# A fixed opening order in which every read of one PSUM bank comes ahead of the tile that takes the bank over

## The chip, the cores and the metric

The kernel runs on one core of one Trainium2 chip. The metric is device time in microseconds (us) of one execution, by the median of several runs. The core has a matmul engine (PE, with PEld for its weight loads), a vector engine (DVE), an activation engine (ACT), GpSimd (POOL) and SyncE (SP), which here only issues DMAs. Each engine works its own instructions off in the order of the program and stops at an instruction whose inputs are not there yet.

## The reference

Two decoder layers over 512 tokens of width 1024. Each layer is a SwiGLU feed-forward half step, a token mixer (windowed attention, RWKV-7 and a short convolution side by side) and a second feed-forward half step. Each of the six sub-layers starts from a normalised input whose scale and shift come from the conditioning vector `c`:

```python
c_act = jax.nn.silu(c)
mod = (c_act @ w_ada[l] + b_ada[l]).reshape(B, N_MOD, D_MODEL)
hn = rms_norm(h, g_ffn1[l]) * (1.0 + sc1) + sh1
h = h + 0.5 * (1.0 + gt1) * swiglu(hn, w_ffn1_in[l], w_ffn1_out[l])
```

This case is about the very start: the first `rms_norm`, the first scale and shift (`sc1`, `sh1`), and the first products with `w_ffn1_in`. All of that must be computed while the inputs are still arriving from memory.

## The kernel before

Activations lie with features on the 128 partitions and the 512 tokens along the row, so `h` is eight blocks of 128x512, `h[0]` to `h[7]`. Every large product is made to float32 accuracy from three matmuls: operand and weight are split into a high and a low part (`hnH`, `hnL`; `wH`, `wL`), and high by high, low by high and high by low are added up in PSUM. A block `H` is cast on ACT, its rest `L` subtracted on DVE; the same goes for weights.

`begin` writes the opening, up to the sixth output tile of the first feed-forward product. It first loads `cT`, the identity, `h` and parameters on SP, adds up the squares of the eight blocks, and makes from the sum the root `rstd_t` (four columns, one for each 128 tokens). After that a list of tokens, `PLAN`, says word by word what is issued next, and the helper `pin` keeps this order on PE, ACT and DVE. The tokens are:

- `ada k`, `part k`, `col k`, `gm k` (k = 0 to 2): scale and shift of block k by matmuls: products with the streamed `wada` on PE, a copy on ACT, a column sum on PE, two small DVE instructions.
- `d k`, `e k` (k = 3 to 7): the same for block k as two dot products of 128x1024 on DVE (line 1393); `e k` ends with the two small ones.
- `s0`, `s1`: two halves of silu(c), ACT. `W n`: n matmuls on ones whose result nobody reads.
- `R0`: PE spreads the root over all partitions into the PSUM tile `ps_rstd`.
- `z k`: DVE multiplies block k by `ps_rstd` (line 1419). `x k`, `H k`: ACT applies scale and shift and casts. `L k`: DVE.
- `wH n`, `wL n` (n = 0 to 5): ACT and DVE split the weights of output tile n, which arrive as `wfirst`.
- `Pnka`, `Pnkb`, `Pnkc`: a matmul (line 1408) of output tile n with block k: a is hnH by wH, b is hnL by wH, c is hnH by wL. There are 6 x 8 x 3 = 144.

Output tile n lives in a PSUM bank taken in turn from three pairs: `("r0", "r1", "mm")[n % 3]`. `ps_rstd` is the first tile in pair r1, output tile 1 the second, so output tile 4 takes the bank of `ps_rstd` over. Its first matmul, `P40a`, therefore waits until the last reader of `ps_rstd` is done, also where that reader comes later in the list.

Loads of the opening: eight `wada` of 1024 KB (`wa0`, four buffers) and six `wfirst` of 512 KB (five buffers). Below they are called wada 0 to 7 and wfirst 0 to 5. Four of each are asked for at once; the others are asked for by tokens, in this line, and each waits for the user of the buffer that it takes:

```python
more = {"ada0": (fetch, fetch_w), "ada1": (fetch,), "wL0": (fetch_w, fetch), "e3": (fetch,)}
```

wfirst 5 takes the buffer of wfirst 0, whose last reader is `wL0`. wada 7 takes the buffer that `e3` reads last. After the opening, SP sends the rest of the constants and the next weights (`wraw`), and the feed-forward code goes on with output tile 6 (matmuls of lines 127 to 129).

Of the kernel before, what the change touches and what calls it, by code (L numbers as in the profile page):

```python
# [8 lines left out]
F32 = mybir.dt.float32  # L9
F32R = mybir.dt.float32r  # L10
I32 = mybir.dt.int32
AF = mybir.ActivationFunctionType
ALU = mybir.AluOpType
# [4 lines left out]
P = 128  # L18
D = 1024
T = 512  # L20
# [6 lines left out]
NB = T // P  # L27
# [3 lines left out]
BASE = 16  # L31
PAD = 24
PLAN = """
ada0 R0 W1 s0 part0 wH0 col0 z0 gm0 s1 z4 W1 ada1 x0 z3 H0 z2 part1 P00a L0 wH1 col1 z1 P00b wH2 P10a wL1 P10b W1 P20a P20b gm1 P10c wL2 x1 ada2 H1
wL0 P20c part2 P01a P11a wH3 col2 L1 P00c P01c gm2 P30a P30b wL3 x2 P01b P11c P11b P21a H2 P21c d3 P21b P30c P31a P31b P31c P02a L2 P02c P12a P12c e3
P22a P02b P12b P22c P22b wH4 P32a P32c P32b d4 x3 P40a P40b P41a P41b wL4 H3 P42a P42b P03a P03c P13a L3 P40c P41c wH5 P42c z6 P03b P13c P13b e4 P23a
P23c P50a P50b P51a P51b P52a wL5 P52b x4 P23b P33a P33c P33b H4 P43a d6 P50c P51c P52c P43c P43b P53a L4 P53b P53c P04a e6 P04c P04b P14a P14c P14b
P24a P24c d7 x6 P24b P34a P34c P34b H6 P44a P44c z7 P44b P54a P54c L6 P54b P06a P06c e7 P06b P16a P16c P16b P26a P26c P26b z5 P36a x7 P36c P36b P46a
d5 P46c H7 P46b P56a P56c P56b L7 P07a P07c P17a e5 P17c P07b P17b P27a P27c P27b P37a P37c x5 P37b P47a P47c P47b H5 P57a P57c P57b L5 P05a P05c P15a
P15c P05b P15b P25a P25c P25b P35a P35c P35b P45a P45c P45b P55a P55c P55b  # L40
""".split()
GROUPS = ((0, 12), (12, 22))
STEP = 0.65
# [25 lines left out]
def trunk_kernel(ctx, tc, ins, out, layers=L, phases=("ffn1", "mix", "ffn2")):  # L69
# [11 lines left out]
    tt, stt, ts = nc.vector.tensor_tensor, nc.vector.scalar_tensor_tensor, nc.vector.tensor_scalar  # L81
    act, mm = nc.scalar.activation, nc.tensor.matmul

    def E(name="e", dt=F32):
        return sp.tile([P, T], dt, name=name, tag="e", bufs=4)
# [4 lines left out]
    def psum(shape, name, tag="x"):  # L90
        return ps.tile(shape, F32, name=name, tag=tag, bufs=2)
# [60 lines left out]
    h = []  # L152
# [13 lines left out]
    ones = ones_r.bitcast(F32)  # L166
# [11 lines left out]
    def cst(name):  # L178
        a, b = CON[name]
        return con[:, a:b]  # L180
# [56 lines left out]
    def new_ss():  # L237
        return sp.tile([P, T], F32, name="ss", tag="ss")
# [1078 lines left out]
    def begin(pool):  # L1317
# [6 lines left out]
        def pin(e, m):  # L1324

            if e in behind:
                tc.add_manual_dep(m.ins, behind[e].ins.name, ORDER, reason="the opening keeps its order")
            behind[e] = m
            return m
# [17 lines left out]
        def warm(n):  # L1347

            for _ in range(n):
                pin("PE", mm(pw.rearrange("p (a b) -> p a b", b=P), ones_r, wide, start=True, stop=True))  # L1350
# [7 lines left out]
        turned = [psum([P, 4, P], "ps_crep", "r0") for _ in range(2)]  # L1358
        for k in range(KD):
            pin("PE", mm(turned[k // 4][:, k % 4], cT[:, k : k + 1].to_broadcast([P, P]), cst("ident"), start=True, stop=True))  # L1360
        warm(14)
        ss, sqs = new_ss(), {}
        for i in range(KD):
            if i:
                sqs[i] = E("sq")
            if i == 3:
                pin("DVE", tt(sqs[3], h[3], h[3], ALU.mult))
            else:
                pin("ACT", act(sqs[i] if i else ss, h[i], AF.Square))
            if i in (3, 4, 5, 6):  # L1370
                for j in range(1, 4) if i == 3 else (i,):
                    pin("DVE", tt(ss, ss, sqs[j], ALU.add))
        for f in (fetch, fetch_w, fetch, fetch_w, fetch_w, fetch, fetch_w, fetch):
            f()
        pt = psum([P, NB], "ps_ss")
        for n, x in enumerate((sqs[7], ss)):
            for b in range(NB):
                pin("PE", mm(pt[:, b : b + 1], x[:, b * P : (b + 1) * P], ones[:, :1], start=n + b == 0, stop=n == 1, skip_group_check=True))
        warm(2)
        r = pool.tile([P, NB], F32, name="rstd_t", tag="rstd_t")  # L1380
        pin("ACT", act(r, pt, AF.Sqrt, bias=vals["eps"], scale=1.0 / D))
        pin("DVE", nc.vector.reciprocal(r, r))
# [79 lines left out]
    with tc.tile_pool(name="first", bufs=1) as fp:  # L1462
        hn, first = begin(fp)
# [112 lines left out]
```

## Time and profile before

| | us |
|---|---|
| median of three runs | 1818.14 |
| the three runs | 1818.14, 1819.16, 1814.23 |
| the profiled execution | 1821.22 |
| its span, first to last instruction | 1819.2 |
| PE busy in the span | 1778.3 (98%) |
| DVE, ACT, POOL busy | 1349.7, 841.2, 142.5 |
| first matmul of line 1408 | starts at 20.45 |
| first matmul after the opening (line 127) | starts at 69.47 |

The opening covers the first 69.47 us, under 4% of the span. The rest is a dense stream of matmuls. The three runs lie 4.93 us apart. The mean granted clock of PE over the span is 0.992 of full speed.

### The profile page before, as it was taken

The page shows a single profiled execution, that of the slowest core. Times are in us where ns is not written, and L with a number is a line of the kernel's source. Part 1 is how long each engine was busy: PE and PEld are TensorE (multiplying, and loading weights), DVE is VectorE, ACT ScalarE, POOL GpSimd, SP SyncE. Part 2 cuts the span into 40 slices and gives each one's busy share as a digit, 9 for nine tenths or more (in the row PEclk, how much of TensorE's full clock was granted, in tenths as well). Part 3 has the DMA queues.
Part 4 walks back from the last instruction along what each step waited for, and adds up shares of the span by engine and source line. Part 5 has one row for each costly group of instructions (what it writes and reads, how often), then busy time and mean ns, then how long its engine had stood idle before and what let it go on. Part 6 is the DMA issues. An engine that isn't in the chain of part 4 may idle for free.

```text
span 1819.2 us, 33688 instructions
## 1 busy us (share of the span) xinstructions
PE 1778.3 (98%) x13846; PEld 1620.3 (89%) x13846; DVE 1349.7 (74%) x2186; ACT 841.2 (46%) x1295; POOL 142.5 (8%) x227
## 2 busy tenths in 40 slices
PE   6999999999999999999999999999999999999999
PEld 4889899898768999899999989998877798999998
DVE  7488677867777877678888776777686698864862
ACT  6244255365433555155445524543644445533551
POOL 0101100101000000100100010110000000010000
PEclk8999999999999999999999999999999999999999
DMA  8466867713123475977737687773321326774742
GB/s 340 171 185 197 280 194 203 252 53 102 57 83 119 139 207 172 299 184 196 237 119 211 173 283 207 193 223 128 120 59 48 133 87 188 192 234 136 201 140 70
DMA packets 91403, 309.91 MB, mean 170 GB/s; under 512 B 10416, under 2 KB 11184, under 8 KB 90224
## 3 DMA queue, kind: packets, MB, share of 16 engines
q1 hardware_dynamic: 61920, 201.58, 32.8%
q0 software_dynamic: 29328, 106.18, 23.2%
q8 instruction: 108, 1.77, 0.4%
q14 instruction: 47, 0.39, 0.1%
HBM read 303.79 MB, written 3.93 MB: 169 GB/s over the span
## 4 chain that ended last, share of the span: by engine, by line
PE 76%; DVE 12%; DMA 6%; ACT 3%; issue 3%; POOL 0%; SPq 0%; ACTq 0%; DVEq 0%; POOLq 0%
PE ps_mm L127 11%; PE ps_mm L128 11%; PE ps_mm L129 11%; PE ps_d L431 7%; PE ps_d L432 7%; PE ps_d L433 7%; PE ps_f L432 3%; PE ps_f L433 3%; PE ps_f L431 3%; DVE wL L141 2%; DMA wada<-in_wadaT 2%; DVE wada L197 2%; PE ps_g L432 2%; PE ps_g L433 2%; PE ps_g L431 2%
## 5 line engine op out<-in xcount | busy, mean ns | idle before, releaser
L139 ACT CAST wH<-wraw 128x1024 fp32r<-128x1024 f32 (+2 forms) x290 | 263.9, 916 | 483.2 <-PE ps_mm L128 201.3
L141 DVE TENSOR_TENSOR wL<-wraw,wH 128x1024 fp32r<-128x1024 f32 (+2 forms) x290 | 305.9, 1059 | 136.6 <-ACT wH L139 135.4
L129 PE MATMUL ps_mm<-actH,wL 128*128 128x512 f32 (+1 forms) x784 | 281.0, 358 | 1.3 <-DVE wL L141 1.3
L127 PE MATMUL ps_mm<-actH,wH 128*128 128x512 f32 (+1 forms) x784 | 281.4, 359 | 0.6 <-ACT wH L139 0.6
L128 PE MATMUL ps_mm<-actL,wH 128*128 128x512 f32 (+1 forms) x784 | 280.8, 358 | 0.0
L127 PE MATMUL ps_mm<-hnH,wH 128*128 128x512 f32 (+1 forms) x712 | 247.1, 353 | 1.7 <-ACT hnH L289 1.3
L128 PE MATMUL ps_mm<-hnL,wH 128*128 128x512 f32 (+1 forms) x712 | 246.5, 348 | 0.2
L129 PE MATMUL ps_mm<-hnH,wL 128*128 128x512 f32 (+1 forms) x712 | 245.1, 346 | 0.6 <-DVE wL L141 0.6
L431 PE MATMUL ps_d<-comH,wH 128*128 128x256 f32 x816 | 226.4, 277 | 0.8 <-ACT s L457 0.7
L432 PE MATMUL ps_d<-comL,wH 128*128 128x256 f32 x816 | 225.5, 276 | 0.0
L433 PE MATMUL ps_d<-comH,wL 128*128 128x256 f32 x816 | 225.4, 276 | 0.0
L141 DVE TENSOR_TENSOR wL<-sum,wH 128x1024 fp32r<-128x1024 f32 x102 | 125.0, 1226 | 83.7 <-ACT wH L139 83.6
L197 DVE SCALAR_TENSOR_TENSOR wada<-wada,crep 128x1024 f32<-128x1024 f32 x128 | 153.5, 1221 | 37.6 <-DMA wada<-in_wadaT 37.5
L129 PEld LDWEIGHTS ps_mm<-actH,wL 128*128 128x128 f32 x784 | 148.9, 190 | 18.5 <-DVE wL L141 2.1
L127 PEld LDWEIGHTS ps_mm<-actH,wH 128*128 128x128 f32 x784 | 148.9, 190 | 17.4 <-ACT wH L139 1.0
L128 PEld LDWEIGHTS ps_mm<-actL,wH 128*128 128x128 f32 x784 | 149.0, 190 | 16.4
L431 PEld LDWEIGHTS ps_d<-comH,wH 128*128 128x128 f32 x816 | 157.5, 193 | 2.3 <-ACT s L457 2.3
L432 PEld LDWEIGHTS ps_d<-comL,wH 128*128 128x128 f32 x816 | 157.6, 193 | 0.0
L433 PEld LDWEIGHTS ps_d<-comH,wL 128*128 128x128 f32 x816 | 157.6, 193 | 0.0
L139 ACT CAST wH<-sum 128x1024 fp32r<-128x1024 f32 x102 | 106.9, 1048 | 105.0 <-PE ps_f L432 42.4
L127 PEld LDWEIGHTS ps_mm<-hnH,wH 128*128 128x128 f32 x712 | 133.4, 190 | 21.9 <-issue 8.0
L129 PEld LDWEIGHTS ps_mm<-hnH,wL 128*128 128x128 f32 x712 | 135.6, 190 | 13.8 <-DVE wL L141 1.0
(388 smaller groups left out, 3869.8 us busy)
## 6 DMA issues: line engine op xcount, KB each, us to landing
wada<-in_wadaT POOLq DMA_DIRECT2D x128, 512.0 KB, 4.8
wraw<-in_wmi SPq DMA_DIRECT2D x40, 512.0 KB, 3.5
wraw<-in_w2p SPq DMA_DIRECT2D x36, 512.0 KB, 3.9
wraw<-in_w1p SPq DMA_DIRECT2D x32, 512.0 KB, 4.7
wraw<-in_w1o SPq DMA_DIRECT2D x32, 384.0 KB, 5.0
wraw<-in_w2o SPq DMA_DIRECT2D x32, 384.0 KB, 4.5
wraw<-in_w1o SPq DMA_DIRECT2D x32, 320.0 KB, 3.7
wraw<-in_w2o SPq DMA_DIRECT2D x32, 320.0 KB, 3.5
```

Of the source, the lines that this page charges most:

```text
L127: mm(acc, wH, xH, start=start, stop=False)
L128: mm(acc, wH, xL, start=False, stop=False)
L129: latest["large"] = mm(acc, wL, xH, start=False, stop=stop)
L139: nc.scalar.copy(hi, src)
L141: return nc.vector.tensor_sub(lo, src, hi.bitcast(F32))
L197: stt(w, w, 1.0, crep, ALU.mult, ALU.mult, accum_out=out_)
L431: mm(acc, wH, xH, start=start and i + k == 0, stop=False, skip_group_check=True)
L432: mm(acc, wH, xL, start=False, stop=False, skip_group_check=True)
L433: mm(acc, wL, xH, start=False, stop=k == 3, skip_group_check=True)
```

## The change

Only `begin` and its list are touched.

First, `PLAN` is another order of the same tokens. All eight `z` now stand in the first line of the list, ahead of `P40a`; before, `z6`, `z7` and `z5` stood behind it. Weight splits move as well: `wL0` from the 38th place to the 74th, two ahead of `P40a`, and `wL1` and `wL4` far towards the end. The numbers of waste matmuls differ.

Second, the sum of squares. Before, blocks 0 to 6 were added one after the other into `ss` on DVE, and the square of block 7 was added by PE, since the column sums were taken of two tiles into one result. Now DVE adds blocks 1 to 3 to block 0, then 5 to 7 to block 4, then the one to the other, and PE sums one tile. Two of the squares have buffers of their own (`sqs`). 22 waste matmuls stand ahead instead of 14, and the two behind are gone.

```diff
-ada0 R0 W1 s0 part0 wH0 col0 z0 gm0 s1 z4 W1 ada1 x0 z3 H0 z2 part1 P00a L0 wH1 col1 z1 P00b wH2 P10a wL1 P10b W1 P20a P20b gm1 P10c wL2 x1 ada2 H1
...
+ada0 R0 part0 s0 col0 z0 wH0 ada1 gm0 z5 x0 z4 part1 z1 H0 W2 col1 z7 s1 P00a wH1 gm1 z3 x1 L0 W4 P10a ada2 z6 wH2 z2 H1 P00b wL2 P10b P20a part2 P20b
...
-        warm(14)
+        warm(22)
         ss, sqs = new_ss(), {}
+        sqs[0] = ss
         for i in range(KD):
-            if i:
-                sqs[i] = E("sq")
+            if i in (3, 4):
+                x = pool.tile([P, T], F32, name="sqs", tag=f"sq{i}")
+            else:
+                x = E("sq") if i else ss
+            sqs[i] = x
             if i == 3:
-                pin("DVE", tt(sqs[3], h[3], h[3], ALU.mult))
+                pin("DVE", tt(x, h[i], h[i], ALU.mult))
             else:
-                pin("ACT", act(sqs[i] if i else ss, h[i], AF.Square))
-            if i in (3, 4, 5, 6):
-                for j in range(1, 4) if i == 3 else (i,):
-                    pin("DVE", tt(ss, ss, sqs[j], ALU.add))
+                pin("ACT", act(x, h[i], AF.Square))
+        for a, b in ((0, 1), (0, 2), (0, 3), (4, 5), (4, 6), (4, 7), (0, 4)):
+            pin("DVE", tt(sqs[a], sqs[a], sqs[b], ALU.add))
...
-        for n, x in enumerate((sqs[7], ss)):
-            for b in range(NB):
-                pin("PE", mm(pt[:, b : b + 1], x[:, b * P : (b + 1) * P], ones[:, :1], start=n + b == 0, stop=n == 1, skip_group_check=True))
-        warm(2)
+        for b in range(NB):
+            pin("PE", mm(pt[:, b : b + 1], ss[:, b * P : (b + 1) * P], ones[:, :1], start=True, stop=True))
```

Numbers at the end of names below count buffers; in the changed kernel line numbers from 1378 on are one higher.

On PE, around the place where output tile 4 begins. Before (`ps_mm_375` is output tile 4, `ps_mm_335` tile 3, `ps_mm_276` tile 0; `hnH_114` is block 0, `hnH_120` block 3):

```order
L1408 MATMUL ps_mm_335<-hnL_119,wH_324 128x512
L1408 MATMUL ps_mm_375<-hnH_114,wH_367 128x512
L1408 MATMUL ps_mm_375<-hnL_115,wH_367 128x512
L1408 MATMUL ps_mm_375<-hnH_116,wH_367 128x512
L1408 MATMUL ps_mm_375<-hnL_117,wH_367 128x512
L1408 MATMUL ps_mm_375<-hnH_118,wH_367 128x512
L1408 MATMUL ps_mm_375<-hnL_119,wH_367 128x512
L1408 MATMUL ps_mm_276<-hnH_120,wH_243 128x512
```

36 matmuls of line 1408 stand ahead of tile 4's first one and 108 stand from there on; tile 5 follows with 91 from its first one on.

The changed kernel, where output tile 5 (`ps_mm_407`, high weights `wH_396`, made of wfirst 5) begins; `ps_mm_299` is output tile 1, `ps_mm_321` tile 2, `ps_mm_338` tile 3:

```order
L1409 MATMUL ps_mm_284<-hnL_121,wH_250 128x512
L1409 MATMUL ps_mm_299<-hnL_121,wH_286 128x512
L1409 MATMUL ps_mm_407<-hnH_114,wH_396 128x512
L1409 MATMUL ps_mm_407<-hnL_115,wH_396 128x512
L1409 MATMUL ps_mm_407<-hnH_116,wH_396 128x512
L1409 MATMUL ps_mm_407<-hnL_117,wH_396 128x512
L1409 MATMUL ps_mm_407<-hnH_118,wH_396 128x512
L1409 MATMUL ps_mm_407<-hnL_119,wH_396 128x512
L1409 MATMUL ps_mm_321<-hnL_121,wH_312 128x512
```

Tile 4's first matmul has 30 ahead of it now, tile 5's has 47 ahead, and 97 stand from tile 5's first one on.

On SP, the loads that are asked for by tokens. Before:

```order
L1335 DMA wada_231<-in_wa0 128x2048
L1341 DMA wfirst_233<-in_w1i 128x1024
L1335 DMA wada_266<-in_wa0 128x2048
L1341 DMA wfirst_315<-in_w1i 128x1024
L1335 DMA wada_317<-in_wa0 128x2048
L1335 DMA wada_360<-in_wa0 128x2048
L1457 DMA con_83<-in_con 128x1056
```

Now:

```order
L1335 DMA wada_234<-in_wa0 128x2048
L1341 DMA wfirst_236<-in_w1i 128x1024
L1335 DMA wada_262<-in_wa0 128x2048
L1335 DMA wada_363<-in_wa0 128x2048
L1341 DMA wfirst_374<-in_w1i 128x1024
L1335 DMA wada_376<-in_wa0 128x2048
L1458 DMA con_83<-in_con 128x1056
```

wfirst 5 (`wfirst_315` before, `wfirst_374` now) stood ahead of wada 6 and stands behind it now; it still waits for `wL0`.

On DVE in the changed kernel, from the sixth `z` on (`hnL_115`, `hnL_117`, `hnL_119` are the low parts of blocks 0 to 2, `wada_213` is wada 3):

```order
L1420 TENSOR_TENSOR z_291<-h2_87,ps_rstd_223 128x512
L1426 TENSOR_TENSOR hnL_115<-z_248,hnH_114 128x512
L1420 TENSOR_TENSOR z_310<-h6_91,ps_rstd_223 128x512
L1420 TENSOR_TENSOR z_315<-h2_87,ps_rstd_223 128x512
L1432 TENSOR_TENSOR wL_313<-wfirst_207,wH_312 128x1024
L1426 TENSOR_TENSOR hnL_117<-z_273,hnH_116 128x512
L1389 SCALAR_TENSOR_TENSOR gm0_133<-ps_col_330,par_93,gb_130 128x1
L1390 TENSOR_TENSOR sh0_134<-ps_col_330,par_93 128x1
L1432 TENSOR_TENSOR wL_328<-wfirst_211,wH_327 128x1024
L1394 SCALAR_TENSOR_TENSOR wada_213,sc_131<-wada_213,crep_142 128x1024
L1426 TENSOR_TENSOR hnL_119<-z_315,hnH_118 128x512
L1394 SCALAR_TENSOR_TENSOR wada_213,sh_132<-wada_213,crep_142 128x1024
```

`z_315` is the eighth and last `z`; it is the 13th DVE instruction after the root was spread, where before the last one (`z_468`) was the 42nd. `wL0` (`wL_251`) follows three rows after the last one shown.

Behind the opening the engines' orders are the same but for one exchange of neighbours: one weight split (line 141 on DVE, line 139 on ACT) comes ahead of one silu product.

More of the change, by code (lines that the diff above doesn't have):

```diff
@@ L33 @@
 PLAN = """
-ada0 R0 W1 s0 part0 wH0 col0 z0 gm0 s1 z4 W1 ada1 x0 z3 H0 z2 part1 P00a L0 wH1 col1 z1 P00b wH2 P10a wL1 P10b W1 P20a P20b gm1 P10c wL2 x1 ada2 H1
[L35 to L40, printed above, removed]
+ada0 R0 part0 s0 col0 z0 wH0 ada1 gm0 z5 x0 z4 part1 z1 H0 W2 col1 z7 s1 P00a wH1 gm1 z3 x1 L0 W4 P10a ada2 z6 wH2 z2 H1 P00b wL2 P10b P20a part2 P20b
+P01a wH3 col2 L1 P20c P11a gm2 P30a P30b wL3 x2 P01b P11b P21a P21c H2 P21b d3 P31a P30c P31b P31c P02a P12a L2 P22a P22c P32a e3 P02b P12b P22b wH4
+P32c P32b wL0 W1 P40a x3 P40b P41a P41b P42a H3 P42b d4 P00c P01c P02c P03a P03c L3 P13a wH5 P23a P23c P33a e4 P03b P13b P50a P50b P51a P51b P52a wL5
+x4 P52b P23b P33c P33b H4 P43a d5 P43b P50c P51c P52c P53a P53b L4 P53c P04a P04c e5 P14a P04b P14b P24a P24c P24b P34a P34c wL4 x5 P34b P44a P44b
+P54a H5 P54c d6 P54b P40c P41c P42c P43c P44c L5 P05a P05c P15a e6 P05b P15b P25a P25c P25b P35a P35c wL1 P35b x6 P45a P45c P45b P55a H6 P55c d7 P10c
+P11c P12c P13c P14c P15c L6 P55b P06a P06c e7 P06b P16a P16c P16b P26a P26c P26b x7 P36a P36c P36b P46a H7 P46c P46b P56a P56c L7 P56b P07a P07c P07b
+P17a P17c P17b P27a P27c P27b P37a P37c P37b P47a P47c P47b P57a P57c P57b
 """.split()
```

## Prediction

> **What bounds the kernel now.** I read the windows first, cut where the opening's matmuls start, stop, resume and end (columns: length, busy time and instructions of PE, PEld, DVE, ACT and POOL, granted clock, share of the DMA engines, GB/s).
>
> ```profile
> 20.45:31.50 11.05, 11.02 (x61) 8.14 (x61) 11.05 (x20) 8.02 (x12) 0.00 (x0) 1.00 1.02 419
> 31.50:44.00 12.50, 0.03 (x1) 0.03 (x1) 12.50 (x27) 5.19 (x7) 0.00 (x0) 0.62 0.74 301
> 44.00:69.47 25.47, 25.47 (x108) 22.03 (x109) 5.17 (x10) 4.76 (x8) 0.70 (x1) 0.92 0.05 21
> 69.47:1819.20 1749.73, 1725.33 (x13581) 1577.57 (x13579) 1313.38 (x2113) 809.11 (x1250) 141.04 (x220) 1.00 0.56 168
> ```
>
> From 69.47 on PE is busy 1725 of 1750 us: whatever the opening ends earlier should come off the total. Inside the opening PE stands still for 12.5 us. The timeline of PE says for what, and how fast matmuls go otherwise (start, length, instruction, idle time before it and what ended it):
>
> ```profile
> 31.15 0.38 PE L1408 MATMUL ps_mm<-hnL,wH 128*128 128x512 f32 x1
> 44.00 0.77 PE L1408 MATMUL ps_mm<-hnH,wH 128*128 128x512 f32 x1 [12.47 <-DVE z L1419]
> ...
> 69.25 0.38 PE L1408 MATMUL ps_mm<-hnL,wH 128*128 128x512 f32 x1
> 69.47 0.38 PE L127 MATMUL ps_mm<-hnH,wH 128*128 128x512 f32 x1
> ```
>
> The matmul at 44.00 is the first of output tile 4. Its weights had been ready for long; it waits for a `z`, the reader of the bank that it takes. At full clock one matmul follows the other by 0.215 us. DVE meanwhile works without a pause, and shows what each kind costs from start to start:
>
> ```profile
> 31.57 1.22 DVE L1431 TENSOR_TENSOR wL<-wfirst,wH 128x1024 fp32r<-128x1024 f32 x1
> 32.71 0.68 DVE L1425 TENSOR_TENSOR hnL<-z,hnH 128x512 fp32r<-128x512 f32 x1
> 33.31 0.68 DVE L1419 TENSOR_TENSOR z<-h,ps_rstd 128x512 f32<-128x512 f32 x1
> 33.91 1.21 DVE L1393 SCALAR_TENSOR_TENSOR wada<-wada,crep 128x1024 f32<-128x1024 f32 x1
> 35.05 0.08 DVE L1393 DVE_READ_ACCUMULATOR wada<-wada,crep 128x1 f32 x1
> 35.05 0.21 DVE L1388 SCALAR_TENSOR_TENSOR gm<-sc,par,gb 128x1 f32<-128x1 f32 x1
> 35.19 0.15 DVE L1389 TENSOR_TENSOR sh<-sh,par 128x1 f32<-128x1 f32 x1
> 35.26 1.21 DVE L1431 TENSOR_TENSOR wL<-wfirst,wH 128x1024 fp32r<-128x1024 f32 x1
> ...
> 43.17 0.68 DVE L1419 TENSOR_TENSOR z<-h,ps_rstd 128x512 f32<-128x512 f32 x1
> ```
>
> A weight split is 1.14, an `L` or a `z` 0.60, a dot product 1.14, the two small ones 0.21. The last `z` at 43.17 sits behind six dot products. It needs nothing that they make: its own inputs are there from 18 us on, when the first `z` runs (a row below). So the stall is one of order, and the new order takes it away.
>
> **The change part by part.** *The stall.* All eight `z` run ahead of tile 4, which then waits for its weights alone. That takes off 12.5 us of waiting. The question is what is late next. Two candidates are DVE's own chain and the loads, which also fill the queue until about 40 us (DMA share 1.02 and 0.74 above). ACT shows the arrival of the last weights by its waits:
>
> ```profile
> 29.65 1.05 ACT L1429 CAST wH<-wfirst 128x1024 fp32r<-128x1024 f32 x1 [1.88 <-DMA wfirst<-in_w1i]
> 30.61 0.81 ACT L1421 ACTIVATE z<-z,sh,gm 128x512 f32<-128x512 f32 x1
> 31.45 0.62 ACT L1423 CAST hnH<-z 128x512 fp32r<-128x512 f32 x1
> 33.41 1.05 ACT L1429 CAST wH<-wfirst 128x1024 fp32r<-128x1024 f32 x1 [1.34 <-DMA wfirst<-in_w1i]
> ...
> 23.05 0.33 SPq L1341 DMA_DIRECT2D wfirst<-in_w1i  x1
> ...
> wraw<-in_w1i SPq DMA_DIRECT2D x1, 512.0 KB, 3.5
> ```
>
> Loads land in the order of the queue. wfirst 4 is there at 29.65, wfirst 5 at 33.41, with wada 5 between: 1536 KB in 3.76 us. Now wada 6 stands ahead of wfirst 5 too: 2560 KB behind wfirst 4, so 3.76 x 2560/1536 = 6.27 us and a landing at 35.9. That holds if it is asked for in time. It was asked for at 23.05 and now waits for the later `wL0`. The last row of the fence, a load of the same size into an empty queue behind the opening, gives the least delay from issue to landing, 3.5 us: asked for before 32.4, it costs nothing more. wada 7 moves behind it and lands 1024 KB later, at 38.4; its first user runs near 46.
>
> *When `wL0` ends.* DVE has from the first `z` to the end of `wL0`: 8 `z` and 3 `L` (11 x 0.60 = 6.6), 3 weight splits (3.4), 2 dot products (2.3), 4 pairs of small ones (0.8): 13.1 us. The first `z` follows from the sum of squares:
>
> ```profile
> 7.09 3.51 PE L1350 MATMUL ps_warm<-ones_r 128*128 128x512 f32 x14
> 8.04 4.61 DVE L1372 TENSOR_TENSOR ss<-ss,sq 128x512 f32<-128x512 f32 x6
> 12.71 1.05 PE L1378 MATMUL ps_ss<-ones_r,ss 128*128 128x1 f32 x8 [0.37 <-DVE ss L1372]
> 14.35 1.94 PE L1436 MATMUL ps_ada<-wada,cz 128*32 128x256 f32 x16
> 16.21 1.76 PE L1414 MATMUL ps_rstd<-con,rstd_t 128*128 128x128 f32 x8
> 18.02 0.69 DVE L1419 TENSOR_TENSOR z<-h,ps_rstd 128x512 f32<-128x512 f32 x1 [3.69 <-PE ps_rstd L1414]
> 18.82 1.07 PE L1436 MATMUL ps_ada<-wada,cz 128*32 128x256 f32 x16
> ```
>
> Six adds in a chain take 4.61, so 0.8 each against 0.60 for independent work. Seven adds are issued now. They do not alternate: the list has the first chain whole, then the second. Only one joint is independent, so the sum is ready at about 13.3 instead of 12.65. The eight more waste matmuls ahead (3.51/14 = 0.25 each) end at 12.6, inside PE's wait for the sum. Against the longer chain, PE goes straight from the column sums to the `ada` products, with no waste matmuls between (14.35 against 13.76 before); so both follow at 14.4 as before. At the slow clock seen here (1.94 and 1.76) the first `z` starts at about 18.1, and at the fast one (`ada` 1.07, the row at 18.82) up to 1.5 us sooner; more waste matmuls ahead speak a little for the fast one. I take the slow end, since the other only gives slack. ACT keeps DVE waiting once, at the split of weights 2. In front of it ACT has, from the end of `ada0` at 16.4, a table load that is now exposed behind `part0`:
>
> ```profile
> 14.08 1.28 ACT L1416 ACT_TABLE_LOAD   x1
> 15.37 0.60 ACT L1416 ACTIVATE crep<-ps_crep 128x512 f32<-128x512 f32 x1
> 16.35 0.37 ACT L1439 COPY part<-ps_ada 128x256 f32<-128x256 f32 x1 [0.38 <-PE ps_ada L1436]
> ```
>
> Two copies, the table load, two silu halves, three casts of weights, two `x` and one `H` come to 8.0 us with 0.1 us overlap each, so to 24.4, where DVE arrives after 5.8 us of its list at 23.9. So `wL0` ends at 18.1 + 13.1 + 0.5 = 31.7. That is 0.7 us inside the bound.
>
> *The end of the opening.* `wH5` is cast from 35.9 to 36.95, and tile 5's first matmul starts at 37.0. PE gets there earlier: from its first matmul at 21.2 (`H0`, 0.75 later than now because of the table load) it has 47 matmuls (10.1), five waste ones (1.1), `ada2` (1.0), a column sum (0.4) and about 0.9 of short waits, which ends at 34.7. So what the change adds earlier, 0.65 us of add chain and 0.75 us by the table load, is hidden behind a wait of 2.3 us for wfirst 5; with that cover gone it would cost those 1.4 us. From 37.0 on 97 matmuls follow: 97 x 0.2155 = 20.9, to 57.9. DVE keeps ahead. It starts `wL5` at 37.0 and has from there 3 weight splits (3.4), 5 dot products (5.7), 2 pairs of small ones (0.4) and 3 `L` (1.8), to 48.3; `e7` with its pair (1.35) to 49.7; then `x7` and `H7` on ACT (1.6) and `L7` (0.7), to 52.0. Its user, `P07b`, is the 82nd of the 97, at 54.4: 2.4 us of slack. The least slack is at `P40c`, the 34th at 44.1, whose `wL4` ends at 42.4. Against 69.47 that gives 11.6 us.
>
> *The clock.* PE's clock is granted by windows of 3.41 us:
>
> ```profile
> 17.51:20.92 3.41, 2.85 (x29) 1.83 (x28) 2.90 (x7) 2.61 (x6) 0.00 (x0) 1.00 1.05 428
> 126.73:130.15 3.42, 1.81 (x14) 1.43 (x13) 3.42 (x4) 3.01 (x5) 0.00 (x0) 1.00 1.00 224
> 130.15:133.56 3.41, 3.41 (x19) 3.41 (x18) 1.80 (x2) 0.57 (x1) 0.00 (x0) 0.50 0.71 246
> ...
> 505.61:509.03 3.42, 1.56 (x66) 1.50 (x67) 3.35 (x7) 0.21 (x1) 0.00 (x0) 1.00 0.02 5
> 509.03:512.44 3.41, 3.41 (x11) 0.81 (x9) 3.34 (x8) 0.00 (x0) 0.00 (x0) 0.50 0.37 99
> ```
>
> A window in which PE is busy 1.81 or 1.56 us is followed by one at half clock; one with 2.85 is not. A wait of 2.3 us leaves 1.1 busy if it lies in one window. That happens with a chance of (3.41 - 2.3)/3.41 = 0.33 for a window edge anywhere; if an edge cuts the wait, the larger part still exceeds 1.6 us in 0.6 of the cases. So about three in four. It costs half of 3.41: 1.7 us. I take it: 9.9 us.
>
> The Trainium skill, "TensorE: Matmul & The Clock Gate", section "Why this matters for your kernels", asks only that PE have no idle gap of more than about 3 us between bursts of matmuls. By it the wait of 2.3 us would cost no clock, and the sum would be 11.6. The trace disagrees so far: 126.73 to 130.15 holds 1.6 us of idle time in all, and the next window is at half.
>
> *Behind the opening.* One pair of neighbours changes place on DVE and ACT; PE's stream hides both, and I cost it at nothing; without that cover it would be one split of 1.14 us, either way. POOL's store of silu(c) waits for DVE's last `L`:
>
> ```profile
> 49.49 0.70 POOL L1458 DMA_DIRECT2D silu_c<-crep  x1 [45.30 <-DVE hnL L1425]
> ...
> 69.77 0.33 SPq L203 DMA_DIRECT2D crep<-silu_c  x1
> ```
>
> It moves to about 52.3, while the load that reads it back moves from 69.77 to about 59 with the end of the opening. With 3.5 us for the store (the load of its size above) 3 us are left, so it costs nothing; a later `L7` would use that up.
>
> Sum: 1821.22 - 9.9 = 1811.3 for the profiled execution, which lies 3.08 above the median of the runs shown. The median then becomes 1808.2.
>
> **The rivals.** *No slow window*: the wait is cut by a window edge, or does not count. Then 11.6 us come off: 1806.5. *Late weights*: DVE ends `wL0` after 32.4, from short waits that I left out (ACT's chain in front of it is new). Each us beyond moves the landing, tile 5 and the end one for one. Between 1 and 4 us I get 1809.2 to 1812.2. Against it: 0.7 us of slack, and 1.5 more if the early clock is full. *Hardly a change*: DVE, 30 us of work from 18 on, becomes the bound instead of PE; were `L7` 8.6 us later than 52.0, its 16 last matmuls (3.4) would end at 64.0, and from there on the total lies between 1812.7 and 1818. For it speaks that DVE had no pause from 18 to 48 us before; against it, 2.4 us of slack and no work added behind the sum of squares. *Slower*: `wH5` stands ahead of `x4` and all later casts on ACT, so if wfirst 5 comes late, blocks 4 to 7 stop as well. This decides from a landing beyond 35.9 + 9.9 + 5.5 = 51.3 us on, and gives 1824 or more. Nothing in the queue's steady 419 GB/s speaks for it.
>
> **How the numbers follow.** Bound for "same": 0.3% of 1818.14, 5.45 us, about what a measurement of this kernel tells from no change. Forecast (1808.2) 0.50; no slow window (1806.5) 0.25; late weights (near 1810.7) 0.14; hardly a change 0.07; slower 0.04. Faster is the sum of the first three, 0.89; same 0.07; slower 0.04. The range runs from the second case less half the spread of the three runs (1806.5 - 2.5 = 1804.0) to the late end of the third (1812.2, rounded to 1812.5).
>
> **What would show it.** In the changed profile: no wait of PE for a `z`; tile 4 starting near 31; a wait of PE near 35 to 37 for the cast of wfirst 5, which ACT started on landing at 35.9; SP issuing that load near 32; perhaps one window at half clock near 38 to 41; line 127 starting at 58 to 60 instead of 69.47; DVE's last `L` at 52. I am wrong if wfirst 5 lands after 37, if `L7` ends after 56, or if line 127 starts early and the end does not move.

## The result and the profile after

| | us |
|---|---|
| changed kernel, median of 4 runs | 1806.24 (1804.61 to 1807.22) |
| kernel before, median of 4 runs | 1817.16 (1814.23 to 1819.16) |
| ratio, 95% interval | 0.994 (0.9923 to 0.9958) |
| profiled execution, changed | 1807.22, span 1805.5 |
| profiled execution, before | 1821.22, span 1819.2 |

The change takes 10.9 us off by the medians; 9.9 were forecast (1808.2). In three sets of runs that each hold both kernels the difference was 10.9, 13.5 and 9.9 us. All 14 runs of the changed kernel together have a median of 1805.9.

The windows of the changed kernel, cut where the opening's matmuls start, where output tile 4 begins, where tile 5 begins and where the opening ends (columns as in the prediction):

```profile
19.37:31.09 11.72, 9.88 (x57) 7.39 (x56) 10.12 (x20) 7.39 (x11) 0.00 (x0) 1.00 1.01 417
31.09:37.33 6.24, 3.94 (x17) 3.13 (x17) 3.22 (x9) 2.38 (x4) 0.00 (x0) 1.00 1.01 414
37.33:60.06 22.73, 22.73 (x97) 19.62 (x98) 15.41 (x28) 8.62 (x13) 0.70 (x1) 0.92 0.20 78
60.06:1805.45 1745.39, 1722.63 (x13581) 1574.29 (x13579) 1312.47 (x2112) 808.83 (x1249) 141.05 (x220) 1.00 0.57 168
```

The opening ends at 60.06 instead of 69.47, so 9.4 of the 13.7 us between the two spans are in it. The other 4.3 us lie in the last row (1745.4 against 1749.7), with 13581 matmuls in both. I don't count that row as a gain of the change: in the ten profiles of the experiments it lies between 1742.2 and 1746.6, and at 1742.9 and 1746.6 in two that keep the old list or nearly so (below). A part of it is the clock: behind the opening three windows of 3.41 us lie at half clock in the profile before (from 130.15, 509.03 and 1396.49 on) and two in the changed one (from 498.44 and 1382.49 on), which makes 1.7 us of the 4.3.

The timeline of PE shows the starts of tile 4, of tile 5 and of the next product:

```profile
31.09 0.48 PE L1409 MATMUL ps_mm<-hnH,wH 128*128 128x512 f32 x1 [0.36 <-ACT wH L1430]
...
34.43 0.59 PE L1409 MATMUL ps_mm<-hnL,wH 128*128 128x512 f32 x2
37.33 0.52 PE L1409 MATMUL ps_mm<-hnH,wH 128*128 128x512 f32 x1 [2.31 <-ACT wH L1430]
...
60.06 0.38 PE L127 MATMUL ps_mm<-hnH,wH 128*128 128x512 f32 x1
```

The wait of 12.47 us for a `z` is gone; tile 4 now waits 0.36 us for the cast of its weights. What is late next is tile 5's cast, by 2.31 us. The timelines of ACT and of SP's queue say why:

```profile
29.99 1.05 ACT L1430 CAST wH<-wfirst 128x1024 fp32r<-128x1024 f32 x1 [2.73 <-DMA wfirst<-in_w1i]
36.24 1.04 ACT L1430 CAST wH<-wfirst 128x1024 fp32r<-128x1024 f32 x1 [3.83 <-DMA wfirst<-in_w1i]
...
23.87 0.33 SPq L1335 DMA_DIRECT2D wada<-in_wa  x1
24.29 0.38 SPq L1341 DMA_DIRECT2D wfirst<-in_w1i  x1
```

wfirst 5 is there at 36.2, 6.25 us behind wfirst 4, and was asked for right behind wada 6. DVE's timeline, at its first square, the last add of the sum of squares, the root, the first `z`, the split of weights 2, a wait for a column sum, `wL0` and the last `L`:

```profile
6.68 0.69 DVE L1371 TENSOR_TENSOR sqs<-h 128x512 f32<-128x512 f32 x1 [5.65 <-DMA h<-in_xT]
...
11.74 0.69 DVE L1375 TENSOR_TENSOR ss<-ss,sqs 128x512 f32<-128x512 f32 x1
13.87 0.18 DVE L1383 RECIPROCAL rstd_t<-rstd_t 128x4 f32<-128x4 f32 x1 [1.44 <-ACT rstd_t L1382]
...
15.67 0.69 DVE L1420 TENSOR_TENSOR z<-h,ps_rstd 128x512 f32<-128x512 f32 x1 [1.56 <-PE ps_rstd L1415]
...
22.43 1.22 DVE L1432 TENSOR_TENSOR wL<-wfirst,wH 128x1024 fp32r<-128x1024 f32 x1 [0.26 <-ACT wH L1430]
...
25.47 0.22 DVE L1389 SCALAR_TENSOR_TENSOR gm<-ps_col,par,gb 128x1 f32<-128x1 f32 x1 [1.22 <-PE ps_col L1444]
...
29.89 1.22 DVE L1432 TENSOR_TENSOR wL<-wfirst,wH 128x1024 fp32r<-128x1024 f32 x1
...
51.62 0.69 DVE L1426 TENSOR_TENSOR hnL<-z,hnH 128x512 fp32r<-128x512 f32 x1 [1.53 <-ACT hnH L1424]
```

### The profile page after: what moved, and what is told of

Read it like the earlier page. It is cut to its first block, busy times and chain, and to the rows that moved or that the text cites. A ratio compares the mean times of both kernels' runs of the same rounds, so it can differ in the third digit from the quotient of the medians.

```text
span 1805.5 us, 33687 instructions
## 1 busy us (share of the span) xinstructions
PE 1774.8 (98%) x13848; PEld 1616.9 (90%) x13848; DVE 1350.3 (75%) x2187; ACT 840.9 (47%) x1295; POOL 142.5 (8%) x227
## 4 chain that ended last, share of the span: by engine, by line
PE 81%; DVE 9%; DMA 4%; ACT 4%; issue 3%; POOL 0%; SPq 0%; ACTq 0%; DVEq 0%; POOLq 0%
PE ps_mm L127 13%; PE ps_mm L128 13%; PE ps_mm L129 13%; PE ps_d L431 7%; PE ps_d L433 7%; PE ps_d L432 7%; PE ps_f L433 3%; PE ps_f L431 3%; PE ps_f L432 3%; PE ps_g L433 2%; PE ps_g L431 2%; PE ps_g L432 2%; DVE wL L141 2%; PE ps_mm L1409 1%; ACT wH L139 1%
## 5 line engine op out<-in xcount | busy, mean ns | idle before, releaser
L129 PEld LDWEIGHTS ps_mm<-actH,wL 128*128 128x128 f32 x784 | 148.7, 190 | 17.5 <-DVE wL L141 0.7
```

What stands on the lines that cost most here:

```text
L129: latest["large"] = mm(acc, wL, xH, start=False, stop=stop)
```

## Experiments

The theory was: the place of the `z`'s in the list makes the whole gain, the landing of wfirst 5 limits it, and a window at half clock behind tile 5's wait may take 1.7 us back. Rivals were a share of the sum of squares, a share of the other moves in the list, and a landing that is no term. The table has what each profile shows, in us; the last column is the median and the number of runs. "wfirst 5 there" is the start of its cast, which in e1 and e3 did not wait for the load, so there the load was in by then. The record of the clock begins between 5.4 and 8.5 us.

| kernel | first `z` | wfirst 5 there | half clock ahead of line 127 | line 127 | behind it | runs |
|---|---|---|---|---|---|---|
| before | 18.02 | 33.4 | 14.1 to 17.5, 34.6 to 48.2 | 69.47 | 1749.7 | 1817.2 (4) |
| changed | 15.67 | 36.2 | 37.6 to 41.1 | 60.06 | 1745.4 | 1806.2 (4) |
| a0, changed again | 15.89 | 36.1 | none | 58.28 | 1745.1 | 1805.1 (5) |
| a1, changed, third | 15.99 | 36.0 | none | 58.13 | 1746.0 | 1805.9 (5) |
| e1, `z`'s only | 18.32 | 33.6 | 12.5 to 22.7 | 57.58 | 1746.6 | 1805.8 (5) |
| e2, squares only | 15.90 | 33.8 | 33.4 to 47.1 | 68.86 | 1742.9 | 1817.6 (10) |
| e5, one `z` late | 16.20 | 35.9 | 35.8 to 52.8 | 74.78 | 1745.4 | 1820.7 (10) |
| e9, list only | 17.35 | 36.3 | 12.7 to 16.1 | 58.43 | 1742.2 | 1806.7 (6) |
| e3, weights first | 15.96 | 33.6 | 21.2 to 31.5 | 59.35 | 1744.1 | 1801.8 (4) |
| e8, the same again | 15.89 | 33.3 | none | 55.47 | 1742.5 | 1800.5 (4) |
| e7, e8 and waste | 16.28 | 33.6 | none | 55.73 | 1743.8 | 1802.3 (4) |
| e4, wait filled | 15.74 | 35.9 | none | 58.12 | 1746.0 | 1805.1 (5) |

Medians of the kernel before beside them: 1818.6 in the set of a0, e1, e3 and e4, 1818.3 in that of e2, e5, e7 and e8, 1815.8 in that of a1 and e9.

**The `z`'s alone.** The kernel before, with three words of its list moved ahead of the weights of tile 4:

```diff
-P22a P02b P12b P22c P22b wH4 P32a ... P42c z6 P03b ... P44a P44c z7 P44b ... P26b z5 P36a
+P22a P02b P12b P22c P22b z5 z6 z7 wH4 P32a ... P42c P03b ... P44a P44c P44b ... P26b P36a
```

> The kernel before with one edit: z5, z6 and z7 stand ahead of wH4, so ahead of tile 4's first matmul; all else, squares included, is as before. Theory (the stall is the bank of the root alone, and wfirst 5 in its old place ahead of wada 6 lands near 33.5): tile 4 starts near 31 to 32, tile 5 does not wait, 108 matmuls x 0.2155 = 23.3 follow, line 127 starts near 55, 14.5 us sooner than before and 5 sooner than in the changed kernel: near 1802. Rival (the rest of the new order is needed to bring DVE's blocks in time): waits for H or L of late blocks, line 127 at 58 to 60, near 1806.

Measured: 1805.82, ratio 0.9924 (0.991 to 0.9937); the unchanged edit beside it, a0, gave 1805.10, 0.9926 (0.9914 to 0.9939).

> The changed kernel once more, beside the experiments on the same chip. Both theories: as the first time, near 1806; line 127 starts near 60, tile 5 waits 2.3 us for the cast of wfirst 5, one window at half clock behind it (unless a window edge cuts the wait: then line 127 near 58.3).

PE's and DVE's timelines of e1:

```profile
33.92 0.45 PE L1408 MATMUL ps_mm<-hnH,wH 128*128 128x512 f32 x1 [0.87 <-DVE z L1419]
...
57.58 0.38 PE L127 MATMUL ps_mm<-hnH,wH 128*128 128x512 f32 x1
...
31.89 1.88 DVE L1419 TENSOR_TENSOR z<-h,ps_rstd 128x512 f32<-128x512 f32 x3
```

Tile 4 waits 0.87 us for the third of these `z`'s instead of 12.47. That gives the gain of the whole change, and no other part is needed for it. The time lies at the rival's number (1806) and not at the theory's (1802), but the rival's mechanism isn't there: from 33.92 to 57.58 PE has no wait for a late block (108 matmuls in 23.66 us). The opening ends later than I expected since 10.2 us at half clock early on (first `z` at 18.32, the matmuls behind it slow) take back what the earlier weights (33.6) give. So it is in part chance that e1 and the changed kernel come out alike: by these profiles e1 loses time to the clock, and the changed kernel to a later load.

**The sum of squares alone.** The kernel before with the seven adds on DVE, one tile summed by PE and 22 waste matmuls, the old list kept.

```diff
-        warm(14)
+        warm(22)
...
-                pin("ACT", act(sqs[i] if i else ss, h[i], AF.Square))
...
+                pin("ACT", act(x, h[i], AF.Square))
+        for a, b in ((0, 1), (0, 2), (0, 3), (4, 5), (4, 6), (4, 7), (0, 4)):
+            pin("DVE", tt(sqs[a], sqs[a], sqs[b], ALU.add))
```

> The kernel before with the new sum of squares and its 22 waste matmuls, the old list kept. Theory (the place of the z's makes the whole gain): PE still stops in front of output tile 4 until the last z that reads the root; DVE may start 2.3 us sooner (first z at 15.7 instead of 18.0), but between its z's stand dot products that wait for their loads, so the last z runs between 40.9 and 43.2; line 127 between 67 and 69.5; time 1816 to 1818.6, at most 2.3 us below the kernel before. Rival (the new sum has a share of its own): the last z and line 127 more than 3 us earlier than before, time under 1815. Second rival (the old chain was as quick): first z at 18.0, time 1818.6.

Measured: 1817.62, ratio 0.9993 (0.9982 to 1.0003). Timelines of DVE and PE:

```profile
15.90 0.69 DVE L1420 TENSOR_TENSOR z<-h,ps_rstd 128x512 f32<-128x512 f32 x1 [1.56 <-PE ps_rstd L1415]
...
43.09 0.68 DVE L1420 TENSOR_TENSOR z<-h,ps_rstd 128x512 f32<-128x512 f32 x1
...
43.91 0.77 PE L1409 MATMUL ps_mm<-hnH,wH 128*128 128x512 f32 x1 [13.83 <-DVE z L1420]
```

The first `z` runs 2.1 us sooner, the last one at the same time as before (43.17). Of the 2.1 us DVE loses 1.25 in three waits that it did not have before (0.36 for a column sum, 0.38 for a `wada` load, 0.51 for the cast of a weight block at 31.13); the rest I did not follow. PE comes sooner and waits longer. A profiled run of 1813.5 looks like a gain, but its opening ends at 68.86; the rest is what lies behind.

**The list alone.** The changed list with the old sum of squares: the second part undone.

```diff
-        for a, b in ((0, 1), (0, 2), (0, 3), (4, 5), (4, 6), (4, 7), (0, 4)):
-            pin("DVE", tt(sqs[a], sqs[a], sqs[b], ALU.add))
...
+            if i in (3, 4, 5, 6):
+                for j in range(1, 4) if i == 3 else (i,):
+                    pin("DVE", tt(ss, ss, sqs[j], ALU.add))
```

> The changed list with the old sum of squares (and its 14 and 2 waste matmuls): the second part of the change undone alone. Theory (the sum of squares gives only slack): the early clock may fall to half as in the kernel before and the first z then starts near 18, but wfirst 5 still lands at 36.2 behind wada 6, tile 5 starts at 37.3, line 127 at 58.2 to 60; time within 1.5 us of the changed kernel, 1804 to 1807. Rival (DVE's chain is tight enough that its start counts): DVE's last L moves from 51.6 to 54 or later, PE waits for it, line 127 and the time later by up to 2.3 us, 1807 to 1808.5.

> The changed kernel once more, as the level for the run beside it and as a third profile of the wait in front of tile 5. Theory (whether that wait is followed by a half-clock window depends on where the windows' edges fall): wait 2.3 to 2.7 us again; a half-clock window after it if one window holds 1.6 us or more of it, and then line 127 near 60, else near 58.2; time 1805 to 1806.3. Rival (the window after it in the first profile was chance of another sort): half clock without such a window, or none with one.

Measured: 1806.72, ratio 0.9949 (0.9937 to 0.9961), beside 1805.86, 0.9949 (0.9936 to 0.9962) for the changed kernel (a1). DVE's and PE's timelines of the list alone:

```profile
10.47 1.49 DVE L1372 TENSOR_TENSOR ss<-ss,sq 128x512 f32<-128x512 f32 x2
13.63 0.18 DVE L1382 RECIPROCAL rstd_t<-rstd_t 128x4 f32<-128x4 f32 x1 [1.68 <-ACT rstd_t L1381]
...
17.35 0.69 DVE L1419 TENSOR_TENSOR z<-h,ps_rstd 128x512 f32<-128x512 f32 x1 [3.48 <-PE ps_rstd L1414]
...
14.29 1.93 PE L1436 MATMUL ps_ada<-wada,cz 128*32 128x256 f32 x16
16.15 1.16 PE L1414 MATMUL ps_rstd<-con,rstd_t 128*128 128x128 f32 x8
...
37.39 0.48 PE L1408 MATMUL ps_mm<-hnH,wH 128*128 128x512 f32 x1 [2.31 <-ACT wH L1429]
```

The root is there 0.24 us sooner than in the changed kernel, though DVE's first square began 0.07 us later (6.75 against 6.68), so the way to the root is about 0.3 us quicker with the old sum. The adds alone are 0.5 us quicker: from that square to the end of the last add it is 5.21 us (to 11.96) instead of 5.75 (to 12.43). The first `z` is 1.7 us later all the same (3.48 us from the root instead of 1.56). PE spreads the root at full clock (1.16 us) but begins with it at 16.15 instead of 14.47, since two more waste matmuls stand ahead and they and `ada0` (1.93 us instead of 1.07) run at half clock. Tile 5 doesn't see any of it: the load sets 37.39. Together with e2, the sum of squares is worth nothing that these runs can tell.

**One `z` back.** The changed kernel with a single word moved:

```diff
-H0 W2 col1 z7 s1 P00a ... x6 P45a P45c P45b P55a H6 P55c d7 P10c
+H0 W2 col1 s1 P00a ... x6 P45a P45c P45b P55a H6 P55c z7 d7 P10c
```

> The changed kernel with one word of its list moved back: z7 stands just ahead of d7 again, behind output tile 4. Theory (tile 4 waits for the last reader of the bank, wherever it stands): PE stops in front of tile 4 from 31 until z7 is done, near 47; the loads land as before, so nothing else is late then; line 127 near 58.2 + 16 = 74, less up to 2 us that the wait of tile 5 hid; time 1805.1 + 14 = 1819 to 1822, slower than the kernel before. Rival (the other seven z's ahead give most of it, the wait is for them together): line 127 near 60 and time within 3 us of the changed kernel, 1805 to 1808.

Measured: 1820.71, ratio 1.0011 (0.9999 to 1.0023). Its timelines of PE and DVE:

```profile
47.43 0.76 PE L1409 MATMUL ps_mm<-hnH,wH 128*128 128x512 f32 x1 [17.03 <-DVE z L1420]
...
74.78 0.38 PE L127 MATMUL ps_mm<-hnH,wH 128*128 128x512 f32 x1
...
46.61 0.68 DVE L1420 TENSOR_TENSOR z<-h,ps_rstd 128x512 f32<-128x512 f32 x1
```

Seven of the eight early give nothing: PE waits 17.03 us for the one that is left. The opening grows by 16.5 us over a0. Tile 4 starts 16.4 us later than there (47.43 against 30.99). Tile 5's wait of 2.3 us is hidden by that, but 47.43 to 52.84 runs at half clock, 5.4 us that hold 2.7 us of work at full clock, so the two nearly cancel. In the kernel before the same holds from 44.00 to 48.23. So in these two kernels a long wait cost its length and 2.1 to 2.7 us behind it.

**The landing of wfirst 5.** It is asked for ahead of wada 6, at `wL2`:

```diff
-        more = {"ada0": (fetch, fetch_w), "ada1": (fetch,), "wL0": (fetch_w, fetch), "e3": (fetch,)}
+        more = {"ada0": (fetch, fetch_w), "ada1": (fetch,), "wL2": (fetch_w,), "e3": (fetch,), "wL0": (fetch,)}
```

> The changed kernel, with wfirst 5 asked for at wL2 and so ahead of wada 6 in the queue; wada 7 is asked for at wL0. Theory (the landing of wfirst 5 sets the end of the opening): it lands 2.5 us sooner, near 33.7, the wait of tile 5 falls from 2.3 to under 0.4 us, no half-clock window follows it, line 127 starts near 56 instead of 60: near 1802. Rival (DVE's chain of dot products and low parts sets the end): line 127 stays at 58 or later, near 1805, with waits of PE for a low part.

> The kernel that asks for wfirst 5 ahead of wada 6, once more, for a second profile and five more runs. Theory (two levels, by whether half-clock windows fall into the opening): runs near 1801.4 where none does, with line 127 at 56, and near 1805 where they do, with line 127 at 59. Rival (the weights' landing is no term): all runs near 1805, the level of the changed kernel.

Measured: 1801.75, ratio 0.9913 (0.9899 to 0.9926), and the second time 1800.51, 0.9907 (0.9891 to 0.9924). ACT's timeline, the windows and PE's timeline of the second:

```profile
33.33 1.05 ACT L1430 CAST wH<-wfirst 128x1024 fp32r<-128x1024 f32 x1 [1.35 <-DMA wfirst<-in_w1i]
...
33.30:55.47 22.17, 22.17 (x104) 19.23 (x103) 16.19 (x32) 9.72 (x14) 0.70 (x1) 1.00 0.39 158
...
55.47 0.38 PE L127 MATMUL ps_mm<-hnH,wH 128*128 128x512 f32 x1
```

wfirst 5 lands 2.8 us sooner than in a0, PE has no wait left behind 33.30, and the opening ends at 55.47, 2.8 us before a0. The first profile shows the same landing and no gain in the opening: three windows at half clock, 21.2 to 31.5, took it back. So the landing is a term, shown by e8's profile, and in the set with a0 the medians differ by 3.3 us; the runs of the two overlap (1800.6 to 1805.2 and 1803.0 to 1806.6). This one line makes the quickest kernels of the study by the medians.

**Keeping the clock.** Two edits fill PE's waits with waste matmuls. In the kernel with the weights first, seven instead of two ahead of the column sum of block 1 and five ahead of `ada2`; in the changed kernel, ten ahead of tile 5:

```diff
-z1 H0 W2 col1 z7 s1 P00a ... L0 W4 P10a ada2 z6
+z1 H0 W7 col1 z7 s1 P00a ... L0 W4 P10a W5 ada2 z6
```

> The same with more waste matmuls in the two early waits of PE: seven instead of two ahead of the column sum of block 1, and five new ones ahead of ada2. Theory (the windows at half clock from 21 to 31 came from those two waits of 1.1 and 0.9 us): no half-clock window between 15 and 56, wfirst 5 landing at 33.6, no wait of PE for it, line 127 at 56.0, every run near 1801. Rival (the waits there aren't the cause, or the waste gets in the way of real work): half-clock windows as before or the first matmuls of line 1409 later by up to 1 us, and runs spread over 1801 to 1805.

```diff
-e4 P03b P13b P50a P50b
+e4 P03b P13b W10 P50a P50b
```

> The changed kernel with ten waste matmuls right ahead of tile 5's first one: the wait for wfirst 5 stays, but PE works through 2.2 us of it. Theory (the half-clock window comes from PE's idle time): tile 5 still starts near 37.3, no window at half clock behind it, line 127 near 58.3, 1.7 us sooner than the changed kernel: near 1804.5. Rival (a wait under 3 us does not touch the clock, and the window at half speed had another cause): a window at half clock there all the same, line 127 near 60, 1806.

Measured: 1802.30, ratio 0.9909 (0.9894 to 0.9925) for the first and 1805.12, 0.9931 (0.9919 to 0.9944) for the second. Windows of the first, then PE's timeline of the second:

```profile
16.90:20.30 3.40, 3.34 (x28) 2.18 (x17) 2.84 (x9) 3.39 (x6) 0.00 (x0) 1.00 1.04 422
20.30:23.70 3.40, 3.38 (x27) 2.04 (x25) 3.14 (x7) 3.23 (x5) 0.00 (x0) 1.00 1.01 416
```

```profile
34.51 2.45 PE L1350 MATMUL ps_warm<-ones_r 128*128 128x512 f32 x10
37.11 0.45 PE L1409 MATMUL ps_mm<-hnH,wH 128*128 128x512 f32 x1
```

In both PE is busy where it stood still, and the opening has no half clock. Neither is told apart from the kernel without the waste: e8 had none either and gave 1800.5, and a0, whose wait was not filled, had none and gave 1805.1. Nor did filling the waits bring the runs together: the first spreads from 1799.2 to 1804.5, e8 from 1799.7 to 1804.0. Both edits stay inconclusive on the time.

## Why the prediction was right, and where not

*The stall.* Right, and shown from both sides: the `z`'s alone give all (e1), and one `z` back takes all away (e5). One reading was off without touching the sum: the rows from 31.57 to 43.17 hold five dot products ahead of the last `z`, not six.

*What is late next.* Right in its size. wfirst 5 lands 6.25 us behind wfirst 4 (6.27 forecast), at 36.2 (35.9), and tile 5 starts at 37.33 (37.0) after a wait of 2.31 us (2.3). DVE's last `L` is at 51.62 (52.0). e8, where it lands 2.8 us sooner and the opening ends 2.8 us sooner than in a0, shows that this load sets the end.

*When `wL0` ends.* This step was wrong. I let wfirst 5 wait for `wL0` and be asked for near 32; it was asked for at 24.29. The description of the kernel says that it takes the buffer of wfirst 0, and that is wrong too. By the times it takes the one that comes free first: in the kernel before, that of wfirst 1, whose split ended at 23.02, just ahead of the issue at 23.05; in the changed kernel, that of wfirst 2, whose split ends at 22.43 + 1.22 = 23.65. Behind that it stood in line after wada 6, issued at 23.87. In e3 and e8, where it doesn't stand behind wada 6, it is issued 0.02 and 0.03 us after that split (at 23.97 and 23.91). The profile before spoke against the step already: `wL0` ended at 25.49 there, 2.4 us behind the issue. The forecast didn't suffer, because the queue and not the issue sets the landing, but the rival of late weights, with its margin of 0.7 us, had no ground. `wL0` itself ended at 29.89 + 1.22 = 31.11, near the 31.7 forecast, but by errors that largely cancel: DVE began its list 2.4 us sooner, and stood still for 2.04 us in it (0.56 and 1.22 for column sums, 0.26 for the cast of weights 2) where 0.5 was forecast.

*The first `z`.* Forecast 18.1, measured 15.67. The longer add chain was a real cost, near its size: 0.5 us between the changed kernel and e9, 0.65 forecast. The clock was mis-sized: I took half clock for `ada0` and the root. The nine profiles with 22 waste matmuls ahead show no half clock between 12.5 and 17.5, the three with 14 each show a window of it there. The number ahead was never changed without the sum of squares, so these runs don't tell which of the two does it. As forecast, none of it reaches the end.

*The clock.* The term of 1.7 us has the right size and the wrong chance. Where the half-clock window came, line 127 started at 60.06 (59.6 forecast); where it didn't, at 58.28, 58.13 and 58.43. It came in one of four profiles with this wait; I had said three in four. Windows around the wait in the changed kernel, then in a0, a1 and e9:

```profile
34.22:37.64 3.42, 1.11 (x5) 0.67 (x4) 0.58 (x5) 1.40 (x2) 0.00 (x0) 1.00 1.00 407
37.64:41.06 3.42, 3.42 (x9) 2.69 (x8) 3.42 (x5) 0.98 (x2) 0.00 (x0) 0.50 0.82 322
```

```profile
32.04:35.45 3.41, 2.88 (x14) 2.18 (x12) 2.14 (x7) 0.26 (x1) 0.00 (x0) 1.00 1.01 414
35.45:38.87 3.42, 1.63 (x8) 1.44 (x9) 1.65 (x2) 2.38 (x3) 0.00 (x0) 1.00 1.01 402
38.87:42.28 3.41, 3.41 (x17) 3.01 (x16) 3.41 (x8) 0.70 (x1) 0.00 (x0) 1.00 0.47 184
```

```profile
32.79:36.20 3.41, 2.00 (x10) 1.41 (x8) 1.44 (x5) 0.21 (x1) 0.00 (x0) 1.00 1.02 419
36.20:39.61 3.41, 2.52 (x12) 2.23 (x13) 2.54 (x4) 2.17 (x3) 0.00 (x0) 1.00 1.02 405
```

```profile
33.15:36.56 3.41, 1.93 (x9) 1.34 (x8) 1.44 (x5) 0.26 (x1) 0.00 (x0) 1.00 1.02 417
36.56:39.98 3.42, 2.59 (x12) 2.29 (x13) 2.61 (x4) 2.12 (x3) 0.00 (x0) 1.00 1.02 405
```

The window with the whole wait (1.11 busy) was followed by half clock. The three waits that an edge cuts were not, although a0's larger part left only 1.63 busy. So the case that I had put at a quarter, without such a window, with line 127 at 57.9 and a median of 1806.5, is the more usual one (line 127 at 58.13 to 58.43), and the median of all 14 runs, 1805.9, lies nearer to it than to 1808.2. By the rule of the Trainium skill that I weighed against it ("TensorE: Matmul & The Clock Gate", section "Why this matters for your kernels": no gap of more than about 3 us) the sum was that same 1806.5. Three profiles agree with it; the first, half clock behind 2.31 us of idle time, does not.

*Behind the opening.* Costed at nothing; right as far as it can be seen. The 4.3 us that the two first profiles differ by there are no more than profiles of other kernels of this study differ by.

## What to carry to other kernels

When a pool takes buffers or banks in turn, look for the last reader of the old tile in each engine's order: one read left behind costs the whole wait, and seven of eight moved cost as much as none. Once such a stall is gone, the next price is read from the order of the load queue, by bytes ahead of the load, and a one-line swap there took off some 3 us more by the medians of the one set of runs that holds both. Split the traces at the place where the edit ends before you credit it: here the rest of the program differed by up to 7.5 us between profiles, for reasons that these runs show only in part (windows at half clock).

## What was not expected of the hardware

Busy time of a window does not settle the clock of the next. Two windows of PE at the same stage of the list, in the changed kernel and in e3:

```profile
17.15:20.56 3.41, 2.27 (x11) 1.51 (x11) 2.85 (x7) 3.41 (x6) 0.00 (x0) 1.00 1.03 420
```

```profile
17.81:21.22 3.41, 2.26 (x11) 1.51 (x10) 2.85 (x8) 3.41 (x7) 0.00 (x0) 1.00 1.01 413
21.22:24.63 3.41, 2.55 (x18) 0.86 (x18) 3.07 (x5) 1.99 (x3) 0.00 (x0) 0.50 1.04 428
24.63:28.05 3.42, 3.42 (x10) 2.92 (x11) 0.35 (x3) 1.35 (x3) 0.00 (x0) 0.50 1.02 418
28.05:31.46 3.41, 3.41 (x9) 2.69 (x8) 3.41 (x5) 2.45 (x3) 0.00 (x0) 0.50 1.01 416
```

The first of each holds 2.27 and 2.26 us of busy time, in 11 matmuls. The one in the changed kernel was followed by full clock, the one in e3 by three windows at half, the last of them behind a window in which PE was busy throughout. With a0's 1.63 us followed by full clock, no bound on the busy time fits all rows; what decides stays open. That it goes by the phase of the windows, which shifts from run to run, is argued from these rows and not shown.
